# A hybrid SSD and GLA layer: tanh of a convolved tile and a chunk's decays issued behind other reads, with four buffers for one tag

## The chip, the core and the metric

One core of one Trainium2 chip runs the whole kernel in one launch. The metric is device time in microseconds (us) of one execution; the kernel before was timed in three runs. The engines are called as the profile calls them: PE (TensorE), DVE (VectorE), ACT (ScalarE), POOL (GpSimd) and SP (SyncE, which here only issues transfers).

## What is computed

One layer over 16 meta tokens and 2048 real tokens of width 1024. Cut to what matters:

```python
u = rmsnorm(h, norm_w)
z, xbc, dt_raw, q, k, v, g_gla, a_lr, merge_g = split_cols(u @ w_in, IN_WIDTHS)
# SSD branch: 4 groups of 4 heads of 64, state 128
xbc = silu(causal_depthwise_conv(xbc, conv_w, conv_b))          # 4 taps over time
xs, bm, cm = split_cols(xbc, ...)
dt = softplus(dt_raw + dt_bias)
# in chunks of 128 tokens, da_cum = cumsum(dt * a):
decay  = exp(where(causal, da_cum[t] - da_cum[s], -inf))
y_diag = einsum((C B^T) * decay, dt, x)
y_off  = C @ state * exp(da_cum)        # state carried from chunk to chunk
y_ssd  = rmsnorm((y + d_skip * xs) * silu(z))
# GLA branch: 4 heads, log decays from a rank-16 projection
log_a = log_sigmoid(a_lr @ gla_gate_w2 + gla_gate_b) / 16
y_gla = rmsnorm(gla_chunked(q, k, v, log_a)) * silu(g_gla)
# merge
merged = sum_b sigmoid(merge_g[b]) * (branch[b] @ w_branch[b])
out = rmsnorm(h + merged @ w_out, final_norm_w)
```

## The kernel before

All products are fp32 in three passes: each operand is kept as a high part and a rest, and `accum` (L189 to L191) issues high x high, high x rest and rest x high. ACT makes the high part of a weight tile (`whl`, L176), POOL or DVE the rest (L177).

The first stage (to about 1506 us of the span) walks over 4 blocks of 512 tokens; block 0 also carries the 16 meta tokens, so that its tiles have 528 columns in two segments of 264, each with a PSUM bank of its own, where the later blocks have 512 columns in one bank. In each block come 4 SSD groups and then 4 GLA heads. An SSD group (`ssd_proj`) projects z and then four tiles of x, B and C. For each of these *convolved tiles*, PE fills one or two banks of the tag `pj` (three banks in all); ACT reads a bank twice, into `cin` (L513, the raw columns) and into `acc` (L514, the last tap and the bias); DVE adds the three other taps (L518), ACT takes tanh (L521), DVE makes silu of it (L522, `act`).

Beside the projections run generators, one step of each for each tile (`step()`): `ssd_scan`, `gla` and others. Three of them matter here.

- `ssd_scan` works through the four chunks of a group. `before(c)` transposes on PE (L580), reads the bank three times on DVE (L583, L585, L586) and once on ACT (L589), and makes the chunk's decay matrix `dm` (tag `sq`): four clamped differences on DVE (L592, from `cb`, a row of cumulated logs that an ACT-queued transfer spreads over the partitions, L531), Exp on ACT (L594), a product with the scores on DVE (L595). `after(c)` multiplies on PE with `dm` (L604) and the state (L605), adds the state (L611) and the outputs (L613, L616 to L618).
- `gates` starts in group 1 of each block. In two steps, for two heads each, PE multiplies the rank-16 gates with `w2` (L473); DVE and ACT each read every bank (L475 into `tok`, L476 into `g_all`). These are *the decay projection's reads*. In block 0 four banks are read in a step, two of them `pj` and two `pt`; later two.
- `load_u` starts after the SSD groups of a block and brings in the next: eight tiles `xt` by SP (L313), squared on ACT (L314), then eight tiles `xk` by SP (L333), scaled on DVE (L253) and split into `u` (L257 on ACT, L262 on DVE).

The tag `acc` serves the convolution, `xt` and `xk` in turn and has two buffers. PE and SP work through their instructions in the order in which the program is written (a manual schedule); ACT, DVE and POOL get theirs from a scheduler. All engines work in order: an instruction that waits holds what stands behind it.

The second stage multiplies gates, branches and output in Strassen-like sums (banks `psa`, `psb`, `psc`). In it POOL issues 32 transfers that add to a tensor in memory (`m<-io`, L966); such transfers keep their descriptors in a piece of on-chip memory that the program sets aside.

Of the kernel before, what the change touches and what calls it, by code (L numbers as in the profile page):

```python
# [7 lines left out]
F32 = mybir.dt.float32  # L8
# [3 lines left out]
AF = mybir.ActivationFunctionType  # L12
ALU = mybir.AluOpType

P = 128
D = 1024
KT = 8
META = 16
BLK = 512
# [6 lines left out]
NSQ = 5  # L26
NT4 = 5
NACT = 8
# [12 lines left out]
def trunk_kernel(ctx: ExitStack, tc: tile.TileContext, xm, xmt, w_feat, w_tok, w_zm, w_br, w_o,  # L41
                 cf32, cmsk, pvec, fnw, hvec, gw2, out):
    nc = tc.nc
# [84 lines left out]
    wk = first.enter_context(tc.tile_pool(name="wk", bufs=2))  # L128
# [175 lines left out]
    def load_u(b):  # L304
        row0 = META + b * BLK
        uh, ul = u_pair(BLK)

        def rows_rstd(r0, n):
            ss = mk(sm, [P, 1], F32, "ss")
            s2 = mk(sm, [P, 2], F32, "ss2")  # L310
            for i in range(2):
                xt = mk(wk, [P, META + BLK], F32, "acc")[:, :BLK]
                nc.sync.dma_start(xt, xm[r0:r0 + n, i * BLK:(i + 1) * BLK])  # L313
                nc.scalar.activation(xt, xt, AF.Square, accum_out=s2[:, i:i + 1])  # L314
            nc.vector.tensor_tensor(ss, s2[:, 0:1], s2[:, 1:2], op=ALU.add)
            r = mk(sm, [P, 1], F32, "rs1")
            nc.vector.tensor_scalar(r[:n], ss[:n], 1.0 / D, EPS, op0=ALU.mult, op1=ALU.add)
            nc.gpsimd.tensor_tensor(r[:n], r[:n], mhalf[:n, 0:1], op=ALU.pow)
            return r

        rs = []
        for c in range(NCH):
            rs.append(rows_rstd(row0 + c * P, P))
            yield
        rb = bank(pt, "pt")
        for c in range(NCH):
            nc.tensor.matmul(rb[:, c * P:(c + 1) * P], rs[c].to_broadcast([P, P]), ident, start=True, stop=True)
        rbc = mk(wk, [P, 3 + META + BLK], F32, "cin")[:, :BLK]
        nc.scalar.activation(rbc, rb, AF.Copy)
        yield  # L330
        for kt in range(KT):
            xk = mk(wk, [P, META + BLK], F32, "acc")[:, :BLK]
            nc.sync.dma_start(xk, xmt[:, kt, row0:row0 + BLK])  # L333
            scale_u(kt, xk, rbc)
            to_u(b, kt, xk, uh, ul)
            yield
        return uh, ul
# [22 lines left out]
    nc.scalar.activation(nega, hv[:, 1], AF.Exp)  # L360
    nc.vector.tensor_scalar(nega, nega, -1.0, None, op0=ALU.mult)

    w2r = mk(wk, [P, META + BLK], F32, "acc")[:48, :512]
# [89 lines left out]
    def gates(o):  # L453
        m0, tt, chunks, g_all = o.m0, o.tt, o.chunks, o.g_all
        ast = mk(wk, [P, META + BLK], F32R, "act", bufs=NACT)[:48, :tt]
        for a, n in ([(0, META), (m0, BLK)] if m0 else [(0, BLK)]):
            ps = bank(pt, "pt")
            for i, (ca, cn) in enumerate(chunks):
                if a <= ca < a + n:
                    nc.tensor.transpose(ps[:48, ca - a:ca - a + cn], o.alr[:cn, i], ident[:cn, :cn])  # L460
            nc.scalar.activation(ast[:, a:a + n], ps[:48, :n], AF.Copy)
            nc.vector.tensor_tensor(ast[:32, a:a + n], ps[:32, :n], ast[:32, a:a + n].bitcast(F32),
                                    op=ALU.subtract)
            nc.scalar.activation(ast[:16, a:a + n], ps[:16, :n], AF.Copy)
        yield
        for h2 in range(0, GH, 2):
            gmt = mk(wk, [P, 2, META + BLK], F32, "tok4", bufs=NT4)
            for h in (h2, h2 + 1):
                gm = gmt[:, h % 2, :tt]
                gb = gate_b[:, h:h + 1]  # L470
                for i, (a, n) in enumerate(o.segs_all):
                    ps = bank(*((pt, "pt") if i else (pj, "pj")))
                    nc.tensor.matmul(ps[:, :n], w2[:, h * P:(h + 1) * P], ast[:, a:a + n],  # L473
                                     start=True, stop=True)
                    nc.vector.tensor_scalar(gm[:, a:a + n], ps[:, :n], gb, 0.0, op0=ALU.add, op1=ALU.min)  # L475
                    nc.scalar.activation(g_all[:, h, a:a + n], ps[:, :n], AF.Abs, bias=gb)  # L476
# [12 lines left out]
    def ssd_proj(o, g):  # L489
        m0, tt = o.m0, o.tt  # L490
        feats = []
        zs = mk(wk, [P, NCH, 256], F32, "tok4", bufs=NT4)
        if g == 0:
            pss = [bank(*pl) for pl in [(pj, "pj")] * 3 + [(pt, "pt")] + ([(pc, "pc")] if m0 else [])]
            yield from proj_tok("zm", w_zm, o.u, o.starts + [0] * o.ci0, list(enumerate(pss)), 288, 1, 256)
            begin(dt_chain(o, pss[NCH:] + pss[:NCH]))
            done = [(ps[:, :256], zs[:, c]) for c, ps in enumerate(pss[:NCH])]
        else:
            pss, places = halves_of(pj, "pj")
            yield from proj_tok(f"z{g}", w_tok[g], o.u, o.starts, places)  # L500
            done = [(ps, zs[:, 2 * r:2 * r + 2].rearrange("p c f -> p (c f)")) for r, ps in enumerate(pss)]
        for ps, dst in done:
            nc.scalar.activation(dst, ps, AF.Tanh, scale=0.5)
            nc.vector.scalar_tensor_tensor(dst, dst, 1.0, ps, op0=ALU.add, op1=ALU.mult)
        yield
        for j in range(4):
            ti = g * 4 + j
            pss = proj_feat(f"s{ti}", w_feat[T_SSD + ti], o.segs_all, o.mov)
            cin = mk(wk, [P, 3 + META + BLK], F32, "cin")
            acc = mk(wk, [P, META + BLK], F32, "acc")[:, :tt]  # L510
            nc.scalar.activation(cin[:, 0:3], tails[:, ti, :], AF.Copy)
            for ps, (a, n) in zip(pss, o.segs_all):
                nc.scalar.activation(cin[:, 3 + a:3 + a + n], ps[:, :n], AF.Copy)  # L513
                nc.scalar.activation(acc[:, a:a + n], ps[:, :n], AF.Identity, scale=hcw[:, ti, 3:4],  # L514
                                     bias=hcb[:, ti:ti + 1])
            nc.gpsimd.tensor_copy(tails[:, ti, :], cin[:, tt:tt + 3])
            for k in range(3):
                nc.vector.scalar_tensor_tensor(acc, cin[:, k:k + tt], hcw[:, ti, k:k + 1], acc,  # L518
                                               op0=ALU.mult, op1=ALU.add)
            f = mk(wk, [P, META + BLK], F32, "act", bufs=NACT)  # L520
            nc.scalar.activation(f[:, :tt], acc, AF.Tanh)  # L521
            nc.vector.scalar_tensor_tensor(f[:, :tt], f[:, :tt], 1.0, acc, op0=ALU.add, op1=ALU.mult)  # L522
            feats.append(f)
            yield
        begin(ssd_scan(o, g, feats, zs))

    cbs = {}
# [5 lines left out]
    def ssd_scan(o, g, feats, zs):  # L533
# [28 lines left out]
        for c in range(NCH):  # L562
            a = m0 + c * P
# [6 lines left out]
        held = {}  # L570

        def before(c):
# [14 lines left out]
                                    hb(d_skip[:, hs], P), op=ALU.mult)  # L587
            bt = mk(wk, [P, P], F32, "bt")
            nc.scalar.activation(bt, ps[:, 256:384], AF.Copy)  # L589
            dm = mk(wk, [P, 4, P], F32, "sq", bufs=NSQ)  # L590
            for h in range(4):
                nc.vector.tensor_scalar(dm[:, h], cb[:, h], o.ntc[:, ci, 4 * g + h:4 * g + h + 1], 0.0,  # L592
                                        op0=ALU.add, op1=ALU.min)
            nc.scalar.activation(dm, dm, AF.Exp)  # L594
            nc.vector.tensor_tensor(dm, dm, scm[:, c].unsqueeze(1).to_broadcast([P, 4, P]), op=ALU.mult)  # L595
            held[c] = xdt, xw, bt, dm

        def after(c):
            a = m0 + c * P
# [291 lines left out]
            (nc.gpsimd if very_last else nc.scalar).dma_start(y_left[1][o.b][2 * h + j], gs[j])  # L891


    running, begun = [], []

    def begin(gen):
        begun.append(gen)
# [1 line left out]
    def step():  # L899
        running.extend(begun)  # L900
        begun.clear()
        for gen in list(running):
            if next(gen, running) is running:
                running.remove(gen)

    def beside_unit(key):
        for j in range(4):
# [344 lines left out]
```

## Time and profile before

| | |
|---|---|
| Runs of before | 2311.09, 2300.68, 2314.6 us; median 2311.09 |
| Profiled execution | 2312.58 us, of which the span from first to last instruction is 2310.8 |
| PE busy | 2234.1 us, 97% of the span |
| DVE, ACT, POOL busy | 69%, 49%, 31% |
| Mean granted clock of PE | 0.987 |

An engine's busy time leaves out its waits; a wait is put down to what ended it (its releaser). The granted clock is 1.00 at full speed; stretches at 0.5 appear in the records, most of them some 3.4 us long, and a window's mean clock shows how many it has.

### The profile page before, as it was taken

The page shows a single profiled execution, that of the slowest core. Times are in us where ns is not written, and L with a number is a line of the kernel's source. Part 1 is how long each engine was busy: PE and PEld are TensorE (multiplying, and loading weights), DVE is VectorE, ACT ScalarE, POOL GpSimd, SP SyncE. Part 2 cuts the span into 40 slices and gives each one's busy share as a digit, 9 for nine tenths or more (in the row PEclk, how much of TensorE's full clock was granted, in tenths as well). Part 3 has the DMA queues.
Part 4 walks back from the last instruction along what each step waited for, and adds up shares of the span by engine and source line. Part 5 has one row for each costly group of instructions (what it writes and reads, how often), then busy time and mean ns, then how long its engine had stood idle before and what let it go on. Part 6 is the DMA issues. An engine that isn't in the chain of part 4 may idle for free.

```text
span 2310.8 us, 36292 instructions
## 1 busy us (share of the span) xinstructions
PE 2234.1 (97%) x12599; PEld 1948.2 (84%) x12599; DVE 1604.4 (69%) x3108; ACT 1121.0 (49%) x2508; POOL 705.1 (31%) x709
## 2 busy tenths in 40 slices
PE   6999999999999999999999999899999999999998
PEld 6899888888889989888988898778787788788786
DVE  5787766687765677675578656664668855788876
ACT  5555654463443454444455334454544545554443
POOL 3344433122221122221122100145325364424441
PEclk9999999999999999999999999989999999999999
DMA  7766865667786676786667654475768856779653
GB/s 256 234 214 217 300 230 203 213 193 248 252 270 192 207 231 204 257 285 207 205 217 231 215 163 151 151 227 197 242 231 251 244 189 215 259 247 250 191 187 109
DMA packets 296200, 507.49 MB, mean 220 GB/s; under 512 B 27104, under 2 KB 143072, under 8 KB 296016
## 3 DMA queue, kind: packets, MB, share of 16 engines
q1 hardware_dynamic: 217232, 413.76, 55.4%
q10 hardware_dynamic: 74016, 82.50, 10.3%
q0 software_dynamic: 4768, 8.92, 2.4%
q8 instruction: 99, 1.62, 0.3%
q14 instruction: 85, 0.70, 0.1%
HBM read 357.87 MB, written 147.19 MB: 219 GB/s over the span
## 4 chain that ended last, share of the span: by engine, by line
PE 70%; DMA 10%; DVE 9%; issue 5%; ACT 3%; POOL 2%; SPq 1%; ACTq 0%; POOLq 0%; DVEq 0%
PE pj L189 12%; PE pj L191 12%; PE pj L190 12%; PE psa L189 5%; PE psa L190 4%; PE psa L191 4%; PE psb L191 2%; PE psb L190 2%; PE psb L189 2%; DMA br<-br_t 2%; PE pc L604 2%; PE pc L768 2%; DVE b L989 1%; DMA acc<-in_xmt 1%; POOL whl L177 1%
## 5 line engine op out<-in xcount | busy, mean ns | idle before, releaser
L189 PE MATMUL pj<-u,whl 128*128 128x512 f32 (+1 forms) x1184 | 447.7, 378 | 9.0 <-ACT acc L514 3.9
L191 PE MATMUL pj<-u,whl 128*128 128x512 f32 (+1 forms) x1184 | 432.2, 365 | 0.8 <-POOL whl L177 0.8
L190 PE MATMUL pj<-u,whl 128*128 128x512 f32 (+1 forms) x1184 | 431.6, 365 | 0.0
L189 PE MATMUL pj<-whl,u 128*128 128x256 f32 (+1 forms) x992 | 289.5, 292 | 2.4 <-ACT u L257 2.2
L191 PE MATMUL pj<-whl,u 128*128 128x256 f32 (+1 forms) x992 | 283.0, 285 | 0.2 <-DVE u L262 0.2
L190 PE MATMUL pj<-whl,u 128*128 128x256 f32 (+1 forms) x992 | 282.8, 285 | 0.3 <-POOL whl L177 0.3
L189 PE MATMUL psa<-b,a 128*128 128x512 f32 x640 | 254.4, 397 | 18.1 <-ACT sn L1029 17.9
L189 PEld LDWEIGHTS pj<-u,whl 128*128 128x128 f32 x1184 | 225.9, 191 | 48.4 <-ACT acc L514 4.8
L191 PEld LDWEIGHTS pj<-u,whl 128*128 128x128 f32 x1184 | 225.3, 190 | 37.0 <-POOL whl L177 1.0
L190 PE MATMUL psa<-b,a 128*128 128x512 f32 x640 | 252.9, 395 | 2.0 <-DVE b L989 2.0
L190 PEld LDWEIGHTS pj<-u,whl 128*128 128x128 f32 x1184 | 225.7, 191 | 33.6
L191 PE MATMUL psa<-b,a 128*128 128x512 f32 x640 | 252.3, 394 | 0.0
L1013 DVE TENSOR_TENSOR a<-ar,a 128x512 fp32r<-128x512 f32 x160 | 156.4, 983 | 83.9 <-ACT a L1012 83.1
L80 POOL TENSOR_TENSOR wr<-wr 128x256 f32<-128x256 f32 x80 | 67.1, 838 | 449.7 <-DMA wr<-u 188.0
L177 POOL TENSOR_TENSOR whl<-wr,whl 128x512 fp32r<-128x512 f32 (+1 forms) x100 | 136.4, 1371 | 191.8 <-ACT whl L176 160.8
L189 PEld LDWEIGHTS pj<-whl,u 128*128 128x128 f32 x992 | 190.5, 192 | 4.0 <-ACT u L257 2.3
L190 PEld LDWEIGHTS pj<-whl,u 128*128 128x128 f32 x992 | 190.6, 192 | 0.9 <-POOL whl L177 0.5
L191 PEld LDWEIGHTS pj<-whl,u 128*128 128x128 f32 x992 | 190.4, 192 | 0.8 <-DVE u L262 0.8
L989 DVE TENSOR_TENSOR b<-br,b 128x512 fp32r<-128x512 f32 x196 | 151.9, 798 | 43.9 <-ACT b L988 43.6
L988 ACT ACTIVATE b<-br 128x512 fp32r<-128x512 f32 x196 | 119.0, 626 | 105.6 <-DMA br<-br_t 40.2
L518 DVE SCALAR_TENSOR_TENSOR acc<-cin,hcw,acc 128x512 f32<-128x512 f32 (+1 forms) x192 | 159.6, 831 | 11.7 <-ACT acc L514 9.4
L189 PEld LDWEIGHTS psa<-b,a 128*128 128x128 f32 x640 | 122.2, 191 | 49.0 <-ACT sn L1029 22.9
(285 smaller groups left out, 4930.0 us busy)
## 6 DMA issues: line engine op xcount, KB each, us to landing
whl<-k_s SPq DMA_DIRECT2D x96, 512.0 KB, 4.4
whl<-k_g SPq DMA_DIRECT2D x96, 512.0 KB, 4.2
whl<-k_v SPq DMA_DIRECT2D x48, 512.0 KB, 3.7
whl<-k_z SPq DMA_DIRECT2D x36, 512.0 KB, 4.1
wr<-in_w_feat SPq DMA_DIRECT2D x64, 256.0 KB, 4.4
k_s<-whl SPq DMA_DIRECT2D x32, 512.0 KB, 3.6
cb<-cumd ACTq DMA_DIRECT2D x64, 256.0 KB, 6.0
k_g<-whl SPq DMA_DIRECT2D x32, 512.0 KB, 4.2
```

Source lines behind the costliest of these rows:

```text
L80: nc.gpsimd.tensor_tensor(o, x, y, op=ALU.subtract)
L177: nc.gpsimd.tensor_tensor(hl[:, 1], raw, hl[:, 0].bitcast(F32), op=ALU.subtract)
L189: nc.tensor.matmul(ps, sh, mh, start=first, stop=False, **kw)
L190: nc.tensor.matmul(ps, sh, ml, start=False, stop=False, **kw)
L191: nc.tensor.matmul(ps, sl, mh, start=False, stop=last, **kw)
L518: nc.vector.scalar_tensor_tensor(acc, cin[:, k:k + tt], hcw[:, ti, k:k + 1], acc, op0=ALU.mult, op1=ALU.add)
L604: nc.tensor.matmul(py[:, h * 64:(h + 1) * 64], dm[:, h], xdt[:, h], start=True, stop=True)
L768: nc.tensor.matmul(ps[:, r * P:(r + 1) * P], kq[:, 2 * r * P:(2 * r + 1) * P], kq[:, (2 * r + 1) * P:(2 * r + 2) * P], start=True, stop=True)
L988: nc.scalar.activation(t[:, 0], raw, AF.Copy)
L989: nc.vector.tensor_tensor(t[:, 1], raw, t[:, 0].bitcast(F32), op=ALU.subtract)
L1013: nc.vector.tensor_tensor(t[:, 1], src, t[:, 0].bitcast(F32), op=ALU.subtract)
```

## The change

1. `ssd_proj`: tanh (ACT) and the silu product (DVE) of convolved tile j are no longer issued in the step of tile j but in that of tile j+1, behind tile j+1's last read of its bank on ACT (`tc.issue_after` orders instructions of the engine, it adds no wait). The last tile of a group stays where it was.
2. `acc` gets four buffers in place of two, everywhere.
3. `ssd_scan`: the decays of a chunk (L592, L594, L595) go on a list and are issued at the end of the step, behind the decay projection's last pair of reads where the step has any.
4. The memory set aside for POOL's transfer descriptors goes from the default 16384 to 2048.

```diff
-                xt = mk(wk, [P, META + BLK], F32, "acc")[:, :BLK]
+                xt = mk(wk, [P, META + BLK], F32, "acc", bufs=4)[:, :BLK]
...
-            xk = mk(wk, [P, META + BLK], F32, "acc")[:, :BLK]
+            xk = mk(wk, [P, META + BLK], F32, "acc", bufs=4)[:, :BLK]
...
-                    nc.vector.tensor_scalar(gm[:, a:a + n], ps[:, :n], gb, 0.0, op0=ALU.add, op1=ALU.min)
-                    nc.scalar.activation(g_all[:, h, a:a + n], ps[:, :n], AF.Abs, bias=gb)
+                    ends = (nc.vector.tensor_scalar(gm[:, a:a + n], ps[:, :n], gb, 0.0, op0=ALU.add, op1=ALU.min),
+                            nc.scalar.activation(g_all[:, h, a:a + n], ps[:, :n], AF.Abs, bias=gb))
+            reads.extend(ends)
...
+        owed = []
+
+        def convolved(acc):
+            f = mk(wk, [P, META + BLK], F32, "act", bufs=NACT)
+            nc.scalar.activation(f[:, :tt], acc, AF.Tanh)
+            nc.vector.scalar_tensor_tensor(f[:, :tt], f[:, :tt], 1.0, acc, op0=ALU.add, op1=ALU.mult)
+            feats.append(f)
...
-                nc.scalar.activation(acc[:, a:a + n], ps[:, :n], AF.Identity, scale=hcw[:, ti, 3:4],
-                                     bias=hcb[:, ti:ti + 1])
+                got = nc.scalar.activation(acc[:, a:a + n], ps[:, :n], AF.Identity, scale=hcw[:, ti, 3:4],
+                                           bias=hcb[:, ti:ti + 1])
+            while owed:
+                with tc.issue_after(got.ins):
+                    convolved(owed.pop())
...
-            f = mk(wk, [P, META + BLK], F32, "act", bufs=NACT)
-            nc.scalar.activation(f[:, :tt], acc, AF.Tanh)
-            nc.vector.scalar_tensor_tensor(f[:, :tt], f[:, :tt], 1.0, acc, op0=ALU.add, op1=ALU.mult)
-            feats.append(f)
-            yield
+            owed.append(acc)
+            if j < 3:
+                yield
+        convolved(owed.pop())
+        yield
...
-            dm = mk(wk, [P, 4, P], F32, "sq", bufs=NSQ)
...
-            held[c] = xdt, xw, bt, dm
+
+            def decays():
+                dm = mk(wk, [P, 4, P], F32, "sq", bufs=NSQ)
...
+                held[c] = xdt, xw, bt, dm
+
+            behind.append(decays)
...
     def step():
...
+        with ExitStack() as queue:
+            while reads:
+                queue.enter_context(tc.issue_after(reads.pop().ins))
+            while behind:
+                behind.pop(0)()
...
-    nc = _bacc.Bacc("TRN2", target_bir_lowering=False, num_devices=1)
+    nc = _bacc.Bacc("TRN2", target_bir_lowering=False, num_devices=1, dynamic_dma_scratch_size=2048)
```

No instruction is added or taken away. PE and SP have the same rows in the same order in both kernels. On ACT and DVE the order differs in the first stage, and the places on which most depends are these; line numbers of the changed kernel are higher by up to 16 (L475 and L476 stay, L592 is L606, L594 is L608, L595 is L609, L521 and L522 are L511 and L512).

ACT in block 0, group 0, where the second convolved tile's banks are read (`cin_748` and `acc_749` before, `cin_745` and `acc_746` now). Before:

```order
L176 ACTIVATE whl_850<-wr_852 128x512
L521 ACTIVATE act_667<-acc_657 128x528
L513 ACTIVATE cin_748<-pj_683 128x264
L514 ACTIVATE acc_749<-pj_683,hcb,hcw 128x264
L513 ACTIVATE cin_748<-pj_684 128x264
L514 ACTIVATE acc_749<-pj_684,hcb,hcw 128x264
```

Now:

```order
L176 ACTIVATE whl_847<-wr_849 128x512
L522 ACTIVATE cin_745<-pj_680 128x264
L523 ACTIVATE acc_746<-pj_680,hcb,hcw 128x264
L522 ACTIVATE cin_745<-pj_681 128x264
L523 ACTIVATE acc_746<-pj_681,hcb,hcw 128x264
L511 ACTIVATE act_752<-acc_657 128x528
```

The tanh of the first tile (`act<-acc`) has moved from ahead of the second tile's four reads to behind them.

DVE in block 0, group 1, the first step of `gates`; `tok<-pj,pv` and `tok<-pt,pv` at L475 are the decay projection's reads, `sq<-cb,ntc` are the clamped differences. Before:

```order
L592 TENSOR_SCALAR sq_1105<-cb_991,ntc_366 128x128 x4
L583 TENSOR_TENSOR c_123_1098<-pt_1094,tkd_364 128x256
L585 TENSOR_TENSOR c_124_1100<-pt_1094,wde_367 128x256
L586 TENSOR_TENSOR tok_119_1090<-pt_1094,pv 128x256
L475 TENSOR_SCALAR tok_127_1112<-pj_1113,pv 128x264
L475 TENSOR_SCALAR tok_127_1112<-pt_1117,pv 128x264
L475 TENSOR_SCALAR tok_127_1112<-pj_1121,pv 128x264
L592 TENSOR_SCALAR sq_1309<-cb_993,ntc_366 128x128
L475 TENSOR_SCALAR tok_127_1112<-pt_1125,pv 128x264
```

Now:

```order
L595 TENSOR_TENSOR c_123_1098<-pt_1094,tkd_364 128x256
L597 TENSOR_TENSOR c_124_1100<-pt_1094,wde_367 128x256
L598 TENSOR_TENSOR tok_119_1090<-pt_1094,pv 128x256
L475 TENSOR_SCALAR tok_126_1105<-pj_1106,pv 128x264
L475 TENSOR_SCALAR tok_126_1105<-pt_1110,pv 128x264
L475 TENSOR_SCALAR tok_126_1105<-pj_1114,pv 128x264
L475 TENSOR_SCALAR tok_126_1105<-pt_1118,pv 128x264
L606 TENSOR_SCALAR sq_1124<-cb_991,ntc_366 128x128 x4
L606 TENSOR_SCALAR sq_1329<-cb_993,ntc_366 128x128 x4
```

Four differences that stood at the head now stand behind all four reads. On ACT the Exp that belongs to them (L594) stood ahead of the bank's read L589 and of the four `g_all` reads and now stands behind them. The decays of chunks 2 and 3 of this group, which before followed at once, now come in the second step.

DVE in that second step, block 0, group 1, while the convolved tile `acc_1404` (`acc_1401` now) is worked on. Before:

```order
L518 SCALAR_TENSOR_TENSOR acc_1404<-cin_1403,hcw,acc_1404 128x528
L613 TENSOR_TENSOR c_177_1445<-pc_1435,ecu_368 128x256
L475 TENSOR_SCALAR tok_179_1452<-pj_1453,pv 128x264
L518 SCALAR_TENSOR_TENSOR acc_1404<-cin_1403,hcw,acc_1404 128x528
L611 TENSOR_TENSOR s_ssd<-s_ssd,pc_1441 128x256
L475 TENSOR_SCALAR tok_179_1452<-pt_1457,pv 128x264
L475 TENSOR_SCALAR tok_179_1452<-pj_1461,pv 128x264
L616 TENSOR_TENSOR c_177_1445<-c_177_1445,pc_1435 128x256
L475 TENSOR_SCALAR tok_179_1452<-pt_1465,pv 128x264
```

Now:

```order
L530 SCALAR_TENSOR_TENSOR acc_1401<-cin_1400,hcw,acc_1401 128x528
L629 TENSOR_TENSOR c_175_1435<-pc_1425,ecu_368 128x256
L512 SCALAR_TENSOR_TENSOR act_1407<-act_1407,acc_1280 128x528
L475 TENSOR_SCALAR tok_177_1442<-pj_1443,pv 128x264
L530 SCALAR_TENSOR_TENSOR acc_1401<-cin_1400,hcw,acc_1401 128x528
L627 TENSOR_TENSOR s_ssd<-s_ssd,pc_1431 128x256
L475 TENSOR_SCALAR tok_177_1442<-pt_1447,pv 128x264
L475 TENSOR_SCALAR tok_177_1442<-pj_1451,pv 128x264
L632 TENSOR_TENSOR c_175_1435<-c_175_1435,pc_1425 128x256
L475 TENSOR_SCALAR tok_177_1442<-pt_1455,pv 128x264
L606 TENSOR_SCALAR sq_1461<-cb_1092,ntc_366 128x128 x4
L606 TENSOR_SCALAR sq_1583<-cb_1293,ntc_366 128x128 x4
```

The silu product of the tile before (`act_1407`), which stood a tile earlier, is now ahead of the first read, and the two later chunks' eight differences are behind the last.

More of the change, by code (lines that the diff above doesn't have):

```diff
@@ L361, in trunk_kernel @@
     nc.vector.tensor_scalar(nega, nega, -1.0, None, op0=ALU.mult)
-    w2r = mk(wk, [P, META + BLK], F32, "acc")[:48, :512]
+    w2r = mk(wk, [P, META + BLK], F32, "acc", bufs=4)[:48, :512]
     for i in range(3):
@@ L509, in ssd_proj @@
             cin = mk(wk, [P, 3 + META + BLK], F32, "cin")
-            acc = mk(wk, [P, META + BLK], F32, "acc")[:, :tt]
+            acc = mk(wk, [P, META + BLK], F32, "acc", bufs=4)[:, :tt]
             nc.scalar.activation(cin[:, 0:3], tails[:, ti, :], AF.Copy)
@@ L589, in before @@
             nc.scalar.activation(bt, ps[:, 256:384], AF.Copy)
-            dm = mk(wk, [P, 4, P], F32, "sq", bufs=NSQ)
[L591 to L595, printed above, removed]
-            held[c] = xdt, xw, bt, dm
+            def decays():
+                dm = mk(wk, [P, 4, P], F32, "sq", bufs=NSQ)
+                for h in range(4):
+                    nc.vector.tensor_scalar(dm[:, h], cb[:, h], o.ntc[:, ci, 4 * g + h:4 * g + h + 1], 0.0,
+                                            op0=ALU.add, op1=ALU.min)
+                nc.scalar.activation(dm, dm, AF.Exp)
+                nc.vector.tensor_tensor(dm, dm, scm[:, c].unsqueeze(1).to_broadcast([P, 4, P]), op=ALU.mult)
+                held[c] = xdt, xw, bt, dm
+            behind.append(decays)
         def after(c):
@@ L891, in gla_scan @@
             (nc.gpsimd if very_last else nc.scalar).dma_start(y_left[1][o.b][2 * h + j], gs[j])
-    running, begun = [], []
+    running, begun, reads, behind = [], [], [], []
     def begin(gen):
```

## The prediction

> **What bounds the kernel now.** The page comes first: how full the engines are, and the chain of work that ended last.
>
> ```profile
> PE 2234.1 (97%) x12599; PEld 1948.2 (84%) x12599; DVE 1604.4 (69%) x3108; ACT 1121.0 (49%) x2508; POOL 705.1 (31%) x709
> PE 70%; DMA 10%; DVE 9%; issue 5%; ACT 3%; POOL 2%; SPq 1%; ACTq 0%; POOLq 0%; DVEq 0%
> ```
>
> PE is busy for 2234.1 of 2310.8 us, so 76.7 us are idle, and no order of instructions can bring more than those and what the clock loses. The change touches none of PE's instructions. So the second view is PE's waits, by what ended them (total, times, longest):
>
> ```profile
> PE psa L189 <- ACT sn L1029: 17.9, 11, 3.9
> PE pt L283 <- DVE tok L278: 13.0, 1, 13.0
> PE pc L868 <- DVE s_gla L871: 7.1, 9, 3.0
> PE pj L189 <- ACT acc L514: 3.9, 4, 1.1
> PE pj L189 <- ACT g_all L476: 3.4, 2, 2.4
> PE pc L604 <- DVE c L616: 2.3, 2, 1.4
> PE pj L191 <- POOL whl L177: 0.8, 1, 0.8
> PE pj L189 <- ACT whl L176: 0.8, 1, 0.8
> ```
>
> The two largest lie where the change does nothing: 17.9 us in the second stage and 13.0 at the start. What it aims at is small: 3.9 us of waiting for the second read of a convolved tile (L514) and 3.4 us for the decay projection (L476), 7.3 us or 0.3% of the time. A hundredth of the time is about 23 us and about the least that a measurement of this kernel tells from no change. The third view is the granted clock, since a wait can cost twice:
>
> ```profile
> 75.00:100.00 25.00, 21.56 (x147) 20.30 (x146) 19.07 (x47) 16.34 (x34) 7.30 (x7) 0.86 0.65 215
> 680.00:700.00 20.00, 16.98 (x72) 14.04 (x71) 8.05 (x19) 6.99 (x22) 2.95 (x4) 0.83 0.55 168
> ```
>
> The last columns but two are the clock: 25 us x 0.14 = 3.5 us of full-speed work lost around the first gates step, and 20 x 0.17 = 3.4 us around the end of block 1's GLA heads. Stretches at half speed last some 3.4 us in the records, so each costs about 1.7 us, and the first window has two of them.
>
> **The decays behind the decay projection's reads.** The timeline of all engines around the first gates step of block 0:
>
> ```profile
> 82.12 1.38 DVE L592 TENSOR_SCALAR sq<-cb,ntc 128x128 f32<-128x128 f32 x4
> 83.42 0.41 DVE L583 TENSOR_TENSOR c<-pt,tkd 128x256 f32<-128x256 f32 x1
> 83.53 0.63 ACT L594 ACTIVATE sq<-sq 128x512 f32<-128x512 f32 x1 [2.01 <-DVE sq L592]
> 84.42 0.48 DVE L475 TENSOR_SCALAR tok<-pj,pv 128x264 f32<-128x264 f32 x1
> 84.93 0.48 ACT L476 ACTIVATE g_all<-pj,pv 128x264 f32<-128x264 f32 x1
> 85.46 0.59 PE L189 MATMUL pj<-u,whl 128*128 128x264 f32 x1 [2.45 <-ACT g_all L476]
> ```
>
> PE has waited 2.45 us for the ACT read that began at 84.93, which followed the DVE read of the same bank (84.42), which followed three other reads (from 83.42), which followed the four differences (from 82.12). Without the differences at the head, the whole row of reads begins at 82.12 and not at 83.42: **-1.30 us**. ACT is free for it, since its Exp, the only instruction of ACT in that time, also moves behind. What is late next is the row of reads itself, so 1.15 us of the wait stay. Whether one of the two half-speed stretches goes with it is open. Of the waits of about 1 us for L514 some are followed by such a stretch and some are not, so I take half of one, **-0.85 us** (bounds -1.7 and 0).
>
> [...]
>
> In the later blocks the same move takes place, but PE lists no more than two waits for L476 in all, the one above and one of 1.0 us: nothing there, hidden behind the projections' matmuls.
>
> **The second gates step, and where the decays land.** The other wait for L476 is in the step after; below it two durations (least, median, longest in ns) and the window around:
>
> ```profile
> 113.03 0.48 DVE L475 TENSOR_SCALAR tok<-pj,pv 128x264 f32<-128x264 f32 x1
> 113.54 0.48 ACT L476 ACTIVATE g_all<-pj,pv 128x264 f32<-128x264 f32 x1 [1.00 <-DVE tok L475]
> L522 DVE SCALAR_TENSOR_TENSOR act<-act,acc x64: 673/692/1372, 54.6 to 1316.5; 128x512 f32<-128x512 f32 x48, 128x528 f32<-128x528 f32 x16
> L592 DVE TENSOR_SCALAR sq<-cb,ntc x256: 265/278/1382, 82.1 to 1331.6; 128x128 f32<-128x128 f32 x128
> L595 DVE TENSOR_TENSOR sq<-sq,sq x64: 675/681/693, 87.6 to 1334.0; 128x512 f32<-128x512 f32 x64
> 100.00:150.00 50.00, 47.92 (x368) 46.11 (x367) 43.98 (x92) 30.77 (x75) 23.07 (x21) 0.97 0.61 198
> ```
>
> ACT stood idle for 1.00 us until DVE's read of that bank. The owed silu product now stands ahead of this DVE read, so both reads, and PE behind them, come one product later: **+0.69 us** (bounds 0, if DVE gets there earlier by as much, and 0.69). Behind the four reads stand the decays of two chunks, 8 x 0.278 + 2 x 0.681 = 3.6 us, in a window in which DVE is busy for 43.98 of 50 us. The six idle microseconds cover them, and the work that they push back is wanted by PE a tile later, about 24 x 2 matmuls of 264 columns away. I take nothing; without that cover it is the 3.6 us.
>
> **Tanh behind the next tile's bank reads.** Around the second and third tiles of block 0:
>
> ```profile
> 53.51 0.28 PE L191 MATMUL pj<-u,whl 128*128 128x264 f32 x1
> 53.97 0.63 ACT L521 ACTIVATE act<-acc 128x528 f32<-128x528 f32 x1
> 54.51 0.37 ACT L513 ACTIVATE cin<-pj 128x264 f32<-128x264 f32 x1
> 55.39 0.39 PE L189 MATMUL pj<-u,whl 128*128 128x264 f32 x1 [0.80 <-ACT acc L514]
> 61.57 0.39 ACT L513 ACTIVATE cin<-pj 128x264 f32<-128x264 f32 x1 [1.29 <-PE pj L191]
> 62.47 0.39 PE L189 MATMUL pj<-u,whl 128*128 128x264 f32 x1 [1.01 <-ACT acc L514]
> ```
>
> At 53.97 the tanh stands between PE's end (53.79) and the reads. Behind them, these begin 0.54 us sooner: **-0.54 us**. At 61.57 ACT had been idle for 1.29 us until PE ended, no tanh stood in the way, and PE waited a full 1.01 us. That is the two reads' own length, and the other two waits for L514 (four in all, 3.9 us, none over 1.1) look the same. So of 3.9 us the change reaches 0.54. In block 0 a tanh is delayed by at most a tile's reads; the transposes of `ssd_scan` need the features only after the fourth tile, which stays in place: nothing.
>
> **Four buffers for `acc`.** SP waits for the buffers before the loads of the next block's rows, and a chain runs from there to a late weight tile:
>
> ```profile
> SPq L313 <- DVE act L522: 17.8, 4, 12.1
> 214.03 2.70 DMA acc<-in_xm
> 219.96 5.92 DMA wr<-in_w_feat
> ```
>
> Of these waits the longest, 12.1 us, ends when block 0's last-but-one silu product frees a buffer and the load at 214.03 goes out. Behind it in SP's order stands the raw weight tile of 219.96. With two more buffers the first loads need not wait for that product, and the weights come up to 12 us earlier. The PE waits that hang on them are the two `whl` rows above, 0.8 + 0.8: **-1.6 us** (bounds -1.6 and 0; all that is left of them if another buffer holds SP). In blocks 1 and 2 no PE wait for `whl` is listed.
>
> The L604 waits for L616 (2 times, 2.3 us) sit at the end of blocks 1 and 2's SSD stage, where the last chunk's decays move by a few DVE rows. They may go (-2.3) or have four differences and a product, 4 x 0.278 + 0.681 = 1.8 us, put in front of each (+3.6). I take nothing.
>
> **The smaller memory for POOL's descriptors.** It concerns POOL's queue and the 32 transfers of L966; the landing times are theirs (least, median, longest):
>
> ```profile
> q0 software_dynamic: 4768, 8.92, 2.4%
> DMA to landing us min/median/max: 3.9/6.2/7.9
> 2102.71 4.45 POOL L966 DMA_DIRECT2D m<-io  x5
> 2129.66 1.68 POOL L1003 TENSOR_TENSOR as<-ar,ar 128x512 f32<-128x512 f32 x1 [6.56 <-DMA br<-out_t]
> ```
>
> 4768 packets over 32 transfers and two others make some 140 for each, and up to five transfers are issued within 4.45 us while one takes 6.2 to land. If an eighth of the memory still holds five, it costs nothing; that I take, since 140 packets spread over 16 engines are nine for each. The other end is a rival below.
>
> **The sum.** -1.30 - 0.85 + 0.69 - 0.54 - 1.6 = **-3.6 us**. The profiled execution took 2312.58 us, which makes 2309.0; it lies 1.5 above the median of the runs, 2311.09, so the median to expect is 2307.5, a change of 0.16%.
>
> **The rivals.**
>
> *More goes than the sum says.* The longest waits of the first stage that lie near the `acc` buffers are those of L868 and L799 for the GLA state, behind loads of `xk` into `acc`:
>
> ```profile
> 282.95 0.50 SPq L173
> 283.54 6.26 DMA acc<-in_xmt
> 689.83 0.79 PE L868 MATMUL pc<-s_gla,act 128*128 128x256 f32 x1 [3.02 <-DVE s_gla L871]
> ```
>
> DVE holds the load's scaling (L253) ahead of the state's update, in order. Were the loads out earlier, up to 7.1 us of L868's waits and the 3.4 us of clock around 690 would go: 2307.5 - 10.5 = 2297, or some 2293 if the other waits of this kind have such a stretch behind them too. Against it: before 283.54 SP had just issued L173 and went straight on to the load. It was held by its place in the queue, which does not change, not by a buffer. It needs SP to run ahead by several microseconds through the earlier loads.
>
> *POOL's ring is too small.* If each L966 must wait until the one before has landed, the five of 2102.71 and the three after them take 8 x 6.2 = 50 us and end at 2152, so that the sum of 2129.66, which prepares the output stage, comes some 20 us late; the group of 1785 does the same once more. With POOL's idle time taken off, 15 us at each of two places reach PE: 2307.5 + 30 = 2337. It decides from the point at which the memory holds fewer than two transfers, 280 packets. That is the case on the slower side.
>
> *The change does nothing that can be seen.* All gains are waits of about 1 us in 2311, in block 0 only, and may come back at the next read of a bank: 2311.
>
> *The decays come too late.* DVE in blocks 0 to 3, pushed by 3.6 us at each gates step, holds the state's update and L604 behind it: 4 x 3.6 = 14 us at most, so 2322. Against it stands the DVE idle time in those windows.
>
> **How the numbers follow.** The forecast has a chance of 0.5, nothing to be seen 0.25, more than the sum 0.1, late decays 0.1, the ring 0.05. The single runs of before spread from 2300.68 to 2314.6, 10 below the median and 4 above, which the first two cases (2307.5 and 2311) carry with them: 2297 to 2315. To hold 8 in 10 with the unknown terms, the range goes down to the case of more (2293) and up to that of late decays (2322); only the ring lies outside. Within 1% of 2311 (2288 to 2334) lie all cases but the ring and the far end of the first rival: faster by over 1% 0.05, same 0.89, slower by over 1% 0.06.
>
> **What would show it.** Right: the wait for L476 near 84 falls from 2.45 to about 1.2 us and the one near 113 grows to about 1.7; the wait at 55 falls to 0.3, that at 62 stays at 1.0; no wait for `whl` near 225; SP's longest wait at L313 well under 12 us; L868 still waits for the state near 690. Wrong: new waits of PE for L609 or L523, a POOL that sits idle between its L966 transfers, or clock dips at other places than before, which a few shifted microseconds may bring about and which I can't foresee.

## The result and the profile after

The changed kernel takes 2319.09 us (median of 22 runs, 2309.86 to 2325.77); before took 2307.2 in the runs beside it (22 runs, 2300.68 to 2315.7). The ratio is 1.0043, with a 95% interval of 1.0032 to 1.0054: slower by some 10 us, where 3.6 us faster was forecast. The profiled execution after took 2324.58 us, 5.5 above its median; that of before lies 5.4 above the later median of 2307.2, so the two traces may be set side by side.

Of the page of the changed kernel, the engines and the chain:

```profile
span 2322.4 us, 36308 instructions
PE 2231.6 (96%) x12599; PEld 1946.8 (84%) x12599; DVE 1612.7 (69%) x3108; ACT 1115.9 (48%) x2508; POOL 709.4 (31%) x709
...
PE 68%; DVE 12%; DMA 9%; issue 5%; ACT 3%; POOL 2%; SPq 1%; ACTq 0%; DVEq 0%; POOLq 0%
```

The page counts 36308 instructions against 36292 before; the difference is in semaphore instructions alone. PE is busy as long as before; the span has grown by 11.6 us, and in the chain DVE has gone from 9% to 12%. PE's waits in the changed kernel (total, times, longest), the largest and those that the change can reach:

```profile
PE psa L189 <- ACT sn L1050: 22.1, 12, 3.0
...
PE pc L884 <- DVE s_gla L887: 7.9, 9, 3.0
PE pc L620 <- DVE sq L609: 7.9, 6, 2.3
PE pj L189 <- ACT acc L523: 6.4, 4, 3.6
...
PE pj L189 <- ACT g_all L476: 3.6, 2, 2.8
...
PE pc L620 <- DVE s_ssd L627: 1.0, 1, 1.0
PE pc L624 <- DVE c L632: 0.9, 1, 0.9
```

A wait that was not in the list of before is the largest of the new ones: PE waits six times, 7.9 us, for the decays' product (L609, formerly L595). The waits for the bank reads (L523) have grown from 3.9 to 6.4 us. The waits for `whl` are gone, and so are the two of L604 for L616 (2.3 us); one of 0.9 us for that sum, now L632, stands at another matmul (L624).

PE's instructions are the same in the same order, so each start can be set beside its counterpart. The changed kernel is 1.5 us ahead at 85 us, 2.6 behind at 114, 5.2 behind at 129, 1.4 behind at 300, and loses 1.0 to 2.4 us, 8.8 together, at each of six places (times of before): 481, 506, 842, 866, 1201 and 1225, all of them L620's waits for the decays' product. The second stage begins at 1506.04 in one and 1514.48 in the other, 8.4 us of the 11.6; the rest is a difference in the second stage, where the change moves almost nothing.

### The profile page after: what moved, and what is told of

Read it like the earlier page. It is cut to its first block, busy times and chain, and to the rows that moved or that the text cites. A ratio compares the mean times of both kernels' runs of the same rounds, so it can differ in the third digit from the quotient of the medians.

```text
span 2322.4 us, 36308 instructions
## 1 busy us (share of the span) xinstructions
PE 2231.6 (96%) x12599; PEld 1946.8 (84%) x12599; DVE 1612.7 (69%) x3108; ACT 1115.9 (48%) x2508; POOL 709.4 (31%) x709
## 4 chain that ended last, share of the span: by engine, by line
PE 68%; DVE 12%; DMA 9%; issue 5%; ACT 3%; POOL 2%; SPq 1%; ACTq 0%; DVEq 0%; POOLq 0%
PE pj L189 11%; PE pj L191 11%; PE pj L190 11%; PE psa L189 5%; PE psa L191 5%; PE psa L190 5%; PE psb L189 2%; PE psb L191 2%; PE psb L190 2%; DMA acc<-in_xmt 2%; DMA br<-br_t 2%; PE pc L620 2%; PE pc L784 2%; DVE acc L530 1%; POOL whl L177 1%
## 5 line engine op out<-in xcount | busy, mean ns | idle before, releaser
L80 POOL TENSOR_TENSOR wr<-wr 128x256 f32<-128x256 f32 x80 | 69.6, 870 | 395.2 <-DMA wr<-u 163.5
```

The source lines that it names most:

```text
L80: nc.gpsimd.tensor_tensor(o, x, y, op=ALU.subtract)
```

## The experiments

All ratios are to the kernel before, run on the same chip, with 95% intervals. In each diff the lines stand against the changed kernel, except where it is said otherwise.

### The parts one by one

**The decays alone**: tanh, buffers (at four places) and memory as before.

```diff
-            owed.append(acc)
-            if j < 3:
-                yield
-        convolved(owed.pop())
-        yield
+            convolved(acc)
+            yield
...
-"acc", bufs=4
+"acc"
...
-dynamic_dma_scratch_size=2048
```

> Only part 3 of the change (the decays behind the decay projection's reads); tanh, buffers and descriptor memory as before. Theory 'late decays' (the six waits of PE for the decays' product, 8.8 us together in the changed kernel, and the waits at 94, 114 and 129 in block 0, less the 1.7 us won at 85): 8 to 12 us slower than before, ratio 1.0035 to 1.005, with all six waits for the product in the list of PE. Rival 'owed tanh' (the silu product ahead of the gates reads and the tanh in ACT's queue cost the time): 0 to 3 us slower. Rival 'memory' (descriptor ring or buffers): no change, within 2 us.

Measured: 2319.41 us, ratio 1.0041 (1.0023 to 1.0059). Its list of PE's waits:

```profile
PE pc L617 <- DVE sq L606: 8.2, 7, 1.4
...
PE pj L189 <- ACT acc L523: 5.9, 3, 3.6
```

As the theory of the late decays said, in size and in kind (seven waits where it named six).

**All but the decays**: the one line that puts them on the list is replaced by a call.

```diff
-            behind.append(decays)
+            decays()
```

> Parts 1, 2 and 4 without part 3: decays issued where they were before. Theory 'late decays': 2 to 4 us faster than before (tanh at 55, weights near 225; no wait of PE for the decays' product), ratio 0.998 to 0.9995. Rival 'owed tanh': 6 to 10 us slower, ratio about 1.003 to 1.004. Rival 'memory': 8 to 10 us slower.

Measured: 2316.76 us, ratio 1.0031 (1.0016 to 1.0045). It should have been faster than before by that theory, and it is slower: the theory was only half of it. The tanh costs as well, as the rival had it. The largest of this kernel's waits that the tanh can reach lie in block 0:

```profile
PE pj L189 <- ACT acc L523: 6.8, 4, 4.0
PE pj L189 <- ACT g_all L476: 5.4, 2, 2.8
```

**The buffers and the smaller memory alone**: the call of the second edit, and of the first edit only the lines of the tanh, so that decays and tanh are as before.

> Parts 2 and 4 alone: four buffers for acc and the smaller descriptor memory. Theory 'late decays': 1.5 to 2.5 us faster (the two whl waits near 225 gone, nothing else), ratio about 0.999. Rival 'owed tanh': the same. Rival 'memory': 8 to 10 us slower, ratio about 1.004, with POOL idle between its accumulating transfers or new waits in the second stage.

Measured: 2304.14 us, ratio 0.9977 (0.9965 to 0.9989), faster than before by some 5 us, more than the 1.5 to 2.5 expected. SP's waits for the loads of rows, which were 17.8 and 21.7 us:

```profile
SPq L313 <- DVE act L512: 9.2, 3, 4.1
SPq L313 <- ACT acc L314: 4.8, 3, 2.4
```

The waits for `whl` near 225 are gone, and so are the two for L616. The same kernel was measured once more later; the record lists the same chip number both times:

> The buffers alone, the same kernel as before under that name, on the same chip as the next. If the four buffers really win: ratio 0.9965 to 0.999 again. If the first result was the draw of that chip: 0.999 to 1.001.

Measured: 2306.11 us, ratio 0.9985 (0.9967 to 1.0004). The second interval reaches 1; together the two put the gain at about 0.2%. That it holds on another chip is not shown.

**The smaller memory alone.**

> The smaller descriptor memory alone, two acc buffers, all else as before. Theory: no difference, within 2 us of before (five transfers are issued within 4.5 us in both kernels). Rival 'the smaller memory is what makes the buffers' kernel faster or costs some of it': 2 us or more from before.

Measured: 2308.51 us, ratio 0.9993 (0.9978 to 1.0009). No difference, and POOL issues as it did:

```profile
2102.86 4.46 POOL L984 DMA_DIRECT2D m<-io  x5
```

**The tanh with two buffers**: the decays as before, `acc` without `bufs=4`, default memory.

> Part 1 alone, with two acc buffers and the default descriptor memory. Theory 'late decays': within 2 us of before: 1.0 us won at 55, and perhaps lost again where a tile's buffer is now held longer (its tanh comes later, and the tile after next and the next block's loads wait for it). Rival 'owed tanh': 6 to 10 us slower. Rival 'memory': within 2 us; if two buffers are too few for the owed tanh, 3 us or more slower with waits of PE for the bank reads in every group.

Measured: 2337.14 us (5 runs), ratio 1.0129 (1.0109 to 1.015). All three accounts allowed at most 10 us, save for the clause on two buffers, which foresaw another place. PE and SP in the profiled execution, the slowest of this kernel (2347.79 us):

```profile
PE pj L189 <- DMA whl<-k_g: 9.4, 2, 4.8
...
PE pj L189 <- ACT whl L176: 5.8, 1, 5.8
```

```profile
SPq L313 <- DVE act L512: 24.2, 2, 17.2
```

A tile's `acc` is held until its silu product, which now comes a tile later. SP waits for it up to 17.2 us at the next block's first loads, and the weights behind in SP's queue come late in each block that loads another (PE waits 5.8, 4.8 and 4.6 us near 238, 625 and 990). So the four buffers are what makes the moved tanh bearable.

### Where the decays cost

**Behind the reads in block 0 only**, and **in blocks 1 to 3 only**, both with four buffers and the tanh as before.

```diff
-            behind.append(decays)
+            if o.b == 0:          # the other: o.b > 0
+                behind.append(decays)
+            else:
+                decays()
```

> Four buffers and the smaller memory, tanh as before, decays behind the reads in block 0 only. Theory 'late decays in the later blocks' (six waits of PE for the product in blocks 1 to 3, 8.3 us): nearly all of the loss of the decays lies there, so this is within 2 us of the buffers alone (1.3 to 1.7 us won at 84, as much lost at 94 and 120). Rival 'block 0 carries the loss': 6 to 10 us slower than the buffers alone.

> The counterpart: four buffers and the smaller memory, tanh as before, decays behind the reads in blocks 1 to 3 only. Theory 'late decays in the later blocks': 7 to 10 us slower than the buffers alone, which is 2 to 5 us slower than before, with six waits of PE for the decays' product. Rival 'block 0 carries the loss': within 2 us of the buffers alone.

Measured: block 0 only 2307.3 us, ratio 0.9989 (0.9975 to 1.0004); the later blocks only 2312.45 us, ratio 1.0021 (1.0011 to 1.0032). To the buffers alone (0.9977) the later blocks add 0.44%, some 10 us, block 0 adds 0.12%, which its interval does not tell from nothing. To the second measurement of the buffers (0.9985) it is 0.36% and 0.04%.

**The last chunk's decays in place**, the others behind the reads, in blocks 1 to 3. The lines stand against the kernel of blocks 1 to 3 only.

```diff
-            if o.b > 0:
+            if o.b > 0 and c < NCH - 1:
```

> As the kernel with the decays behind the reads in blocks 1 to 3 only, except that the last chunk's decays stay where they were before. In that kernel PE's six waits for the product are of two kinds: 0.3 to 0.7 us in the first gates step, where twelve differences stand ahead of the first product, and 1.4 to 2.2 us for the last chunk in the second gates step. Theory: the three of the second step go (5 us together), those of the first stay; the time falls by 3 to 6 us, ratio to before 0.9995 to 1.001. Rival 'the place of the decays in the first step costs as much, through DVE as a whole': the time stays within 2 us of that kernel, 1.0015 to 1.0025.

Measured: 2305.36 us, ratio 0.998 (0.9961 to 0.9999), as fast as the buffers alone in the same measurement (0.9985). PE's waits for the product with all of them moved, and with the last chunk left:

```profile
PE pc L620 <- DVE sq L606: 7.2, 6, 2.2
```

```profile
PE pc L620 <- DVE sq L606: 2.7, 3, 1.1
```

Three waits go, 4.5 us, those of the second gates step; the three of the first step stay. By the ratios the time falls by 0.41%, some 9 us, twice the waits and more than was expected. The two intervals, from different chips, leave it between 4 and 14 us, so that the waits may be all of it; whether half speed behind a wait adds to it isn't shown. DVE, ACT, POOL and PE of the changed kernel in that step, in block 1:

```profile
504.92 0.74 DVE L475 TENSOR_SCALAR tok<-pj,pv 128x512 f32<-128x512 f32 x1
505.58 0.40 DVE L632 TENSOR_TENSOR c<-c,pc 128x256 f32<-128x256 f32 x1
505.91 0.86 DVE L606 TENSOR_SCALAR sq<-cb,ntc 128x128 f32<-128x128 f32 x4
506.70 1.23 DVE L530 SCALAR_TENSOR_TENSOR acc<-cin,hcw,acc 128x512 f32<-128x512 f32 x1
507.85 0.96 DVE L633 TENSOR_TENSOR c<-c,tok 128x256 f32<-128x256 f32 x1
508.84 0.83 DVE L634 TENSOR_TENSOR tok<-c,tok 128x256 f32<-128x256 f32 x1
509.59 1.21 DVE L609 TENSOR_TENSOR sq<-sq,sq 128x512 f32<-128x512 f32 x1
...
507.38 0.62 ACT L608 ACTIVATE sq<-sq 128x512 f32<-128x512 f32 x1
...
509.47 0.79 POOL L80 TENSOR_TENSOR wr<-wr 128x256 f32<-128x256 f32 x1
...
510.86 1.10 PE L620 MATMUL pc<-c,sq 128*128 128x64 f32 x8 [2.28 <-DVE sq L609]
```

The last chunk's decays used to be made in the first step; the last product there and its matmul in the trace of before:

```profile
487.06 0.68 DVE L595 TENSOR_TENSOR sq<-sq,sq 128x512 f32<-128x512 f32 x1
...
506.02 1.00 PE L604 MATMUL pc<-c,sq 128*128 128x64 f32 x8
```

They were ready 18 us before PE wanted them. Behind the second step's reads they have only that step left, and between the differences and the product stand three other operations of DVE. ACT's Exp, which stands behind `g_all`, had ended at 508.00, 1.6 us before the product began, so it is DVE's own row that PE waits for, 2.28 us.

That row is also slow. The three operations and the product took 4.23 us; in the rows near 500 the three take 0.74, 0.41 and 0.43, and the median product 0.68, 2.26 together. POOL makes differences of weight tiles for the second stage (L80) meanwhile, and one of them began 0.12 us before the product. In the second steps of blocks 2 and 3 (870 and 1232) the product took 1.21 us too, again 0.12 us behind the start of such a difference, whereas in the kernel before none of the 64 took more than 0.69. So at least 0.5 us of each of these waits goes with the place beside POOL, and "Why the prediction was wrong" shows the same at another product.

### Where the tanh costs

**The GLA copies kept back**: all parts but the decays, and the heads' copies `gl<-g_all` and what hangs on them behind the head's k copy on ACT.

```diff
+        with tc.issue_after(kept.ins):       # the last copy into kf
             nc.scalar.activation(gl[:, :NCH], grc[:, :, P - 1], AF.Copy, scale=ITEMP)
             ...
             nc.scalar.activation(egl, gl[:, :NCH], AF.Exp)
```

> The kernel of all parts but the decays, and beside it every GLA head's small copies of the last column (gl<-g_all), the exponentials that use them and egl are issued on ACT behind the head's k copy, which keeps the scheduler from drawing them ahead of the bank reads of the convolved tiles. Theory 'ACT stands behind the scan' (the tanh moved behind, the scheduler fills the place ahead of the bank reads with copies that wait for DVE's scan, and PE waits 4.0 us at 95): the wait of 4.0 us there falls to about 1 us, and the time falls by 4 to 6 us against that kernel (with the half-speed stretch that follows), to 2 to 4 us above the one with the buffers alone. Rival 'the silu product in DVE's queue is the whole cost': the wait at 95 stays, time within 2 us of the kernel of all parts but the decays.

The kernel of all parts but the decays at the place, ACT and PE:

```profile
95.56 0.20 ACT L737 ACTIVATE gl<-g_all 128x1 f32<-128x1 f32 x1 [1.48 <-DVE g_all L485]
96.76 0.21 ACT L735 ACTIVATE gl<-g_all 128x4 f32<-128x4 f32 x1 [1.00 <-DVE g_all L485]
...
97.11 0.37 ACT L522 ACTIVATE cin<-pj 128x264 f32<-128x264 f32 x1
97.39 0.56 ACT L523 ACTIVATE acc<-pj,hcb,hcw 128x264 f32<-128x264 f32 x1
...
98.00 0.59 PE L189 MATMUL pj<-u,whl 128*128 128x264 f32 x1 [4.01 <-ACT acc L523]
```

And with the copies kept back:

```profile
93.71 0.37 ACT L522 ACTIVATE cin<-pj 128x264 f32<-128x264 f32 x1
...
94.59 0.39 PE L189 MATMUL pj<-u,whl 128*128 128x264 f32 x1 [0.71 <-ACT acc L523]
```

So the reading of the place is right: two small copies, drawn ahead of the bank reads by the scheduler, wait for DVE's scan, and ACT with them; without them PE's wait falls from 4.01 to 0.71 us. But the time did not follow. Measured: 2315.2 us, ratio 1.0037 (1.0023 to 1.0051), beside 1.0031 of the kernel without this edit (on another chip). In the profiled runs the gain holds to the second stage (6.0 us ahead at its start) and is lost in it (1.6 behind at the end), where it has six stretches at half speed to the other's one. Whether that is this kernel or that run, one trace can't tell.

**Tanh behind the next reads in block 0 only**, and **in blocks 1 to 3 only**, with four buffers and the decays as before.

```diff
-            owed.append(acc)
+            if o.b == 0:          # the other: o.b > 0
+                owed.append(acc)
+            else:
+                convolved(acc)
```

> Four buffers and the smaller memory, decays as before, tanh behind the next tile's reads in block 0 only. Theory 'block 0 carries the cost of the tanh' (4.0 us for the bank read at 95 and 2.8 us for the decay projection's read at 115 in the kernel of all parts but the decays, with the half-speed stretches around them, no new wait later): as slow as that kernel, 8 to 12 us above the buffers alone, ratio 1.002 to 1.004 to before. Rival 'the tanh costs in every block' (DVE's silu product later in each group): less than half of it, 2 to 5 us above the buffers alone.

> The counterpart: tanh behind the next tile's reads in blocks 1 to 3 only, where a tile has one bank and PE lists no wait for its reads. Theory 'block 0 carries the cost': within 2 us of the buffers alone, ratio 0.997 to 0.999. Rival 'in every block': 6 to 9 us above the buffers alone, at or above the time of before.

> Tanh behind the next reads in blocks 1 to 3 only, the same kernel again beside the buffers alone. If the tanh costs nothing there, as PE's list of waits says: within 0.0015 of the ratio of the buffers alone in this job. If it costs what the two separate jobs said: 0.002 to 0.004 above it.

Measured: block 0 only 2312.75 us, ratio 1.0019 (1.0004 to 1.0034); later blocks only 2310.03 us, ratio 1.0005 (0.9992 to 1.0018), and again, beside the buffers alone, 2309.72 us, ratio 1.0007 (0.9987 to 1.0026) to their 0.9985. Over the buffers alone block 0 costs about 0.4% and the later blocks 0.2 to 0.3%, twice. The first shows in part as waits at 95 and 115 (3.8 and 2.8 us), with which the profiled execution is 6.7 us behind that of the buffers alone at 120. That execution is the fastest of its twelve (2305.75 us) and has made up for it by 1300, so one trace can't account for the whole. The second was not expected, and its profile shows only small new waits, such as these in block 1:

```profile
494.56 1.10 PE L624 MATMUL pc<-c,sq 128*128 128x64 f32 x8 [1.01 <-DVE s_ssd L631]
516.94 1.96 PE L660 MATMUL pt<-cst,tok 128*128 128x128 f32 x8 [0.76 <-ACT tok L655]
```

They add up to too little, and that profiled execution (2306.17 us) was itself faster than that of the buffers alone (2309.3). That the tanh costs outside block 0 is likely from two measurements, but not shown: in the second, where both kernels ran on one chip, the two intervals overlap. By which waits stays open.

### A version from the readings

**First chunk only, copies kept back**: four buffers, tanh as before, of the decays only block 0's first chunks behind the reads, and the GLA copies kept back.

> The version to which the experiments point: four buffers and the smaller memory, tanh as before, of the decays only those of block 0's first chunk in each group behind the reads (they stand ahead of them before), and the GLA heads' last-column copies kept behind the k copy, so that nothing that waits for the scan stands ahead of the bank reads. Theory 'only the row of reads at 83 is worth it': the wait at 83 falls from 2.4 to about 1.2 us, none of 3.6 us at 95, no wait for the product at 120, and the time is 1 to 4 us below the buffers alone, ratio to before 0.996 to 0.9975. Rival 'what is won in block 0 does not reach the end': within 1.5 us of the buffers alone, or above it.

Measured: 2309.69 us, ratio 1.0001 (0.9988 to 1.0013), the rival's case. The wait at 83 fell as meant and none of 3.6 us followed at 95, but 2.1 us came back at 132, where PE waits for a sum of outputs (L632) that DVE takes up only behind seven pieces of the gates' scan, 4.13 us: the scheduler's order again. The best version stays the four buffers with tanh and decays as they were: it beats before by 0.2% and the changed kernel by 0.6%. The kernel that leaves the last chunk's decays in place is level with it.

## Why the prediction was wrong

The range was 2293 to 2322 and holds 2319; the sign was wrong, and the changed time is near the rival that had a chance of 0.1, the decays that come too late (2322). That nearness is in part luck: the rival counts the decays alone, in all four blocks, while here PE waits for their product in blocks 1 to 3 only, 2.1 to 3.4 us in each, and the loss by the tanh and the gain by the buffers stand beside it. Two of the signs of being wrong that the prediction names came: the waits for L609 are new, and those for L523 grew. It also took some 23 us as about the least change that can be told; the interval over 22 runs reaches 2.5 us to each side. By the steps of the prediction:

- *The decays behind the reads, -1.30 us at 83*: right in kind at that place, and larger: PE's wait there fell from 2.45 to 0.78 us, where about 1.2 was forecast:

```profile
83.97 0.39 PE L189 MATMUL pj<-u,whl 128*128 128x264 f32 x1 [0.78 <-ACT g_all L476]
94.51 0.59 PE L189 MATMUL pj<-u,whl 128*128 128x264 f32 x1 [3.65 <-ACT acc L523]
```

  The second row is what came of it ten microseconds later, the GLA copies ahead of the bank reads. ACT's order there was to be had before the run, and I had read it only at the place where the change aimed.
- *"In the later blocks the same move takes place ...: nothing there, hidden behind the projections' matmuls"*: **this step failed, the one that the experiments show to the end.** I looked for waits that the move could remove, found none and took its price as nothing. The move also makes the product later, and its slack had to be read: from the end of L595 to the L604 that uses it. For the last chunk it was a tile and more (18 us in block 1), and the move used it up. Measured: 7.9 us of waits in the changed kernel; 0.36 to 0.44% over the buffers alone when moved in the later blocks alone, and nothing when the last chunk's stay in place.
- *The second step's silu product, +0.69 us*: the mechanism was right, the size was off. The wait grew to 2.8 us, since the product took 1.78 us:

```profile
113.88 1.78 DVE L512 SCALAR_TENSOR_TENSOR act<-act,acc 128x528 f32<-128x528 f32 x1
115.58 0.48 DVE L475 TENSOR_SCALAR tok<-pj,pv 128x264 f32<-128x264 f32 x1
```

  POOL's row at the same time is a split of a weight tile:

```profile
113.83 1.26 POOL L177 TENSOR_TENSOR whl<-wr,whl 128x512 fp32r<-128x512 f32 x1 [0.77 <-ACT whl L176]
```

  It began 0.05 us earlier and ended at 115.09, and the product needed another 0.57: 1.21 us beside the split and 0.57 behind it, where the usual product is 0.69. In this trace the five silu products that began 0.05 to 0.26 us behind the start of a split took 1.60 to 1.81 us, and the six during which a split began took 0.68 to 0.79. What makes them slow the trace doesn't show. In three other kernels with the tanh moved in block 0 the product at this place takes 1.77 or 1.78 us. I had taken the median of 64 products, 0.692; the longest, 1.372, stood in the same row.
- *Tanh behind the next reads, -0.54 us at 55*: not shown. The wait is gone, but it is absent also in the kernels in which the tanh stands ahead of these reads as before (decays alone and buffers alone), so its going can't be put down to the move. In before, ACT was held ahead of the tanh, at a weight tile; in the decays alone it was not:

```profile
53.44 0.63 ACT L176 ACTIVATE whl<-wr 128x512 fp32r<-128x512 f32 x1 [0.80 <-PE pj L191]
...
52.63 0.62 ACT L176 ACTIVATE whl<-wr 128x512 fp32r<-128x512 f32 x1
```

- *The delayed tanh, "nothing"*: **this step failed too.** The prediction asked only when the transposes need the features, and put the delay itself at nothing. All parts but the decays cost 0.5% over the buffers alone: 4.0 us of waiting at 95, where ACT's row now has the copies that wait for DVE's scan, and 2.8 us for the decay projection's reads. The rest of the 0.5% stays open, and so does how much of it the wait at 95 makes: the time did not fall when that wait was taken away.
- *Four buffers, -1.6 us*: right in place and sign, too small: 3 to 5 us in two measurements. L604's two waits for L616, 2.3 us, which the prediction left at nothing, went too.
- *The memory, nothing*: right, 0.9993 (0.9978 to 1.0009) with the smaller memory alone. That too small a memory makes one transfer wait for another, the rival's case, no run shows.
- *Half speed, -0.85 us*: not there. The window of the first gates step has the same mean clock, 0.86, in the changed kernel:

```profile
75.00:100.00 25.00, 20.48 (x140) 19.01 (x139) 17.82 (x40) 16.49 (x36) 7.89 (x7) 0.86 0.60 198
```

  Up to 1100 us before has seven stretches of 3.4 us, the changed kernel six, in part at other places; in the second stage of the kernels with and without the GLA copies kept back their number was six and one.

The parts do not add: decays +0.41%, buffers -0.2%, tanh over the buffers +0.5% make +0.7%, and all together are +0.43%. Both moved parts meet the same wait at 95 (3.6 us with the decays alone, 4.0 with all but the decays, 3.65 with both) and pay for it once; what is left of the difference lies within the intervals.

## What to carry to other kernels

An instruction that is moved behind others to free a wait has a reader of its own: read the slack from its end to that reader at every place where the move takes effect, not only the wait at the place that it aims at. Where a scheduler orders the engines, an edge at one place lets other instructions forward into the gap, and the whole engine order between the edge and the next wait has to be read again. A late release, such as an owed read of a buffer, wants its buffers counted first: the moved tanh with two cost 1.3% over before, with four 0.3%.

## What was not expected of the hardware

A DVE product of two tiles (`act<-act,acc`) went from 0.69 to 1.78 us when POOL's split of a weight tile, 1.26 us, had begun 0.05 us before it, and a decays' product from 0.68 to 1.21 us behind a shorter one: DVE durations in such a place are not those of the median. The memory for POOL's descriptors could go from the default to 2048 without a difference with five transfers of some 140 packets each issued within 4.46 us (ratio 0.9993). And 3.3 us taken from a wait in the first stage need not show at the end: the second stage took 804.8 us in the profiled run of before and 807.9 in that of the changed kernel, where the change moves almost nothing.
